# Mixture of experts: token rows fetched and returned by indirect transfers, weights as whole 128-row blocks

## The chip, the cores and the metric

The kernel runs on one core of a Trainium2 chip. The metric is the time on the device in microseconds. Three runs of the kernel before gave 1365.46, 1365.88 and 1366.44 us; the median, 1365.88 us, is what the prediction is measured against. The core's engines work side by side: PE multiplies matrices, ACT and DVE work on elements, POOL (GpSimd) does small vector work and issues transfers that need indices, SP issues the others.

## The reference

256 tokens of 1024 numbers go through two transformer blocks. Nearly all of the change lies in the last part, the second block's mixture of experts, and what it computes is this:

```python
logits = (x @ router_w) + router_b
top_vals, top_idx = lax.top_k(logits, TOP_K)                 # TOP_K = 2 of 8 experts
top_w = jax.nn.softmax(top_vals, axis=-1)
gate = jnp.sum(jax.nn.one_hot(top_idx, N_EXPERTS) * top_w[..., None], axis=-2)
out = jnp.zeros_like(x)
for e in range(N_EXPERTS):
    out = out + gate[..., e:e + 1] * ((jax.nn.silu(x @ w1[e]) * (x @ w3[e])) @ w2[e])
x = layer_norm(DEEPNORM_ALPHA * x + out, ln2_g[1], ln2_b[1])
```

w1 and w3 of an expert have 1024 x 1408 numbers, w2 has 1408 x 1024, all of float32; the eight experts' weights are 138.4 MB. Before this part stand an attention block with a dense hidden layer, a second mixer, a second dense hidden layer and a third mixer; the dense layers and mixers are the first 890 us.

## The kernel before

**Weights.** Every weight is streamed once from DRAM. `Weights.load` (L161) takes the next tile of the plan, up to 4 blocks of 128 rows by 512 columns (1 MB), into a free raw slot, by a transfer that SP issues (L171); the expert part has ten such slots (raw, rawx, cpack, rawt). `Weights.convert` (L175) takes a piece of two row blocks by up to 512 columns and splits it into two parts whose products PE can do fast: ACT rounds it to the high part wh (L204), DVE subtracts to get the low part wl (L205). Six pieces of each part fit (`PIECES`, pools wh and wl). `Weights.pump` is called by `tick` after each piece of products and converts the next pieces as far as `free` allows; a raw slot is free again once DVE has made the last low part from it, and SP waits for that.

**Products.** A product of a block of 128 token slots with 512 columns is three matmuls (`mm3`, L375 to L377: x high by w high, x high by w low, x low by w high). For a block of only 64 slots the high and the low parts of x lie side by side in the 128 columns, and two matmuls do (L1473, L1474); their two halves of rows are added up when the hidden columns are turned (`turn`, L1505).

**Experts.** The router ranks each token among its expert's tokens, and the experts but the first are put in order of their number of tokens, falling ("places" 0 to 6). Blocks run in this order: the first expert (None), then places 4, 1, 5, 2, 3, 6, and at the end place 0 together with an extra block, number 8, of its tokens beyond 128, over the same weights. Places 4 to 6 and block 8 have 64 slots (half), the others 128 (full). The first 384 columns of the first expert are computed for all 256 tokens while the router works.

- `gather` (L1421) collects a block's tokens on PE: a 0/1 matrix Pm (token by slot, made by POOL, L1417) is multiplied with x, in 16 matmuls (L1438), each recorded as two rows; the result is split into xgh and xgl. Pm is also transposed to PT (L1456).
- `expert` (L1459) goes through the columns in chunks of 512, 512 and 384: for each chunk w1 (tiles g), then w3 (tiles u), and the hidden columns are transposed on PE (tp) while the next chunk runs. Then w2 runs by halves of 512 output columns (eacc, `down`), and `rows` (L1555, L1556) scales the result by the gate and splits it into yh and yl.
- `combine` (L1594) multiplies PT with yh and yl and so brings each slot back to its token; the sums of all experts stay in four banks comb, eight matmuls for each block (L1600).

**Order.** Nothing reorders the instructions: they stand as the Python code emits them, and every engine takes its own in order. Side tasks such as `gather` are generators that `tick` advances by a step after so many columns of products.

At the end, DVE adds x and the sums, and a layer norm and the store follow.

Of the kernel before, what the change touches and what calls it, by code (L numbers as in the profile page):

```python
# [28 lines left out]
P = 128  # L29
S = 256  # L30
# [19 lines left out]
def _const_pack():  # L50
# [16 lines left out]
    # distances in the retention: keys of the second block backwards, keys of the first forwards  # L67
# [24 lines left out]
class Null:  # L92
    """Stands for everything on the chip while the order of the weight tiles is listed."""
# [19 lines left out]

class Weights:
    """The weights in the order of their use: raw tiles of up to 512 x 512 by DMA, then in pieces of
    two row blocks an exact pair of float32r parts."""

    def __init__(self, b, plan):
        self.b, self.plan = b, plan
        self.pieces, self.where = [], []  # L120
        for i, (name, r0, kt, c0, n, perm, phase) in enumerate(plan or []):
            for k in range(0, kt, 2):
                self.pieces.append((i, k, min(2, kt - k), n, perm))
                self.where.append(phase)
        # slots of a phase: for the last of its pieces (-phase: in its scratch tiles) and every so many before
# [9 lines left out]
        self.left = {i: (t[2] + 1) // 2 for i, t in enumerate(plan or [])}  # L135
        # makers of raw tiles
        self.slots = deque([lambda: b.rawp.tile([P, 4, 512], F32, name="raw")] * RAW_BUFS)
# [4 lines left out]
    def want(self, name, r0, kt, c0, n, perm=False):  # L142
        """The pieces of a tile, which has to be next in the plan."""
        if self.dry:
            self.list.append((name, r0, kt, c0, n, perm, (self.b.nphase, self.b.extra, self.b.tail)))
            return [(min(2, kt - k), Null(), Null()) for k in range(0, kt, 2)]
        out = []
        for k in range(0, kt, 2):
# [12 lines left out]
    def load(self):  # L161
# [4 lines left out]
        raw = raw[:, :kt, :n]  # L166
# [8 lines left out]
    def convert(self):  # L175
# [5 lines left out]
        if self.where[self.nconv] is None:  # L181
            hi, lo = self.b.wh.tile([P, 2, 512], F32R, name="wh"), self.b.wl.tile([P, 2, 512], F32R, name="wl")
# [50 lines left out]
    def free(self):  # L233
        """Whether there is a slot for the next piece."""
        w = self.where[self.nconv]
        if w is not None and abs(w) != self.b.nphase:
            return False
        n = sum(self.where[i] == w for i in range(self.lag, self.nconv))
        if self.nconv - self.lag >= self.b.ahead:
            return False  # L240
        return n < (PIECES if w is None else self.b.extra if w > 0 else self.b.tail)


class Build:
    def __init__(self, tc, ctx, a, out, stop=None, start=None, plan=None):
# [5 lines left out]
        self.wh = pool("wh", PIECES)  # L251
        self.wl = pool("wl", PIECES)
# [3 lines left out]
        self.ps = pool("ps", 8, space=bass.MemoryType.PSUM)  # L256
        ctx.enter_context(tc.manual_schedule())
# [9 lines left out]
    def weight(self, name):  # L267
        """name: (input, indices...), an index may be a place of the experts' order."""
# [38 lines left out]
    def tick(self, work=1.0):  # L307
        """After a piece of the products; the threads go on once per 6144 columns."""
# [70 lines left out]
    def nat_unit(self, ps, x, t, k0, piece, start, stop):  # L379
        """One token tile through one piece."""  # L380
# [52 lines left out]
    def transposed(self, name, c0, n, x, perm=False, kt=KD):  # L433
        """[col, tok] of n columns: a list of banks holding two column tiles of 128 each."""
# [51 lines left out]
    def vec(self, src, name="vec", eng=None):  # L486
        """A row vector in DRAM on all partitions."""
# [73 lines left out]
    def transition(self, gen, acc, finish, T):  # L561
        """The last products of a part; the first token tile goes on while the second is summed."""
# [18 lines left out]
    def setup(self):  # L581
# [7 lines left out]
        if not self.start:  # L589
            # products of no use, so that the tensor engine's clock is up when those of use come  # L590
# [5 lines left out]
            # the row on all partitions  # L596
# [218 lines left out]
    def nextx(self, x):  # L815
        """The transposed input of the next part, made from x."""
# [156 lines left out]
    def decays(self, l):  # L973
        """The logarithms of the decays of both directions; below 0, for distances that stand for a mask."""
# [9 lines left out]
    def mixer(self, l, xT, T, finish, nextT):  # L984
        """The first token tile of xT is there, T(1) makes the second; finish, nextT: see transition."""
# [11 lines left out]
        # retention values, centred within each head  # L997
# [10 lines left out]
        # queries, keys: columns on the partitions  # L1008
        # of the windowed attention, the high and the low parts one above the other
# [26 lines left out]
        # gates of the merge, gates of the retention, output projections  # L1036
# [38 lines left out]
        def gated(j, name, y):  # L1075
            """A half of the columns of an output, transposed, times twice its gate."""
# [122 lines left out]
    def retention(self, tD, rq, rk, rv, sg, yT):  # L1199
# [5 lines left out]
        for hg in range(2):  # L1205
# [41 lines left out]
    def ret_tail(self, hg, y, sg, yT):  # L1247
        """Norms, gates, and the transposed sum of both directions."""
# [50 lines left out]
    def route_top(self, t, ps):  # L1299
        """The two experts of each token of a tile."""  # L1300
# [303 lines left out]
    def moe(self, x, xT, T):  # L1604
# [33 lines left out]
        def between():  # L1638
            self.route_top(0, g[0][:, n0:])
            T(1)  # L1640
# [211 lines left out]
```

## Time and profile before

| | us |
|---|---|
| median of three runs | 1365.88 |
| span of the profiled execution, first to last instruction | 1364.4 |
| busy: PE / DVE / ACT / POOL | 1329.0 / 971.6 / 769.1 / 126.5 |
| the expert part: routing and first expert | 891.66 to 965.29 |
| places 4, 1, 5, 2, 3, 6 | 965.29 to 1260.41 |
| place 0 and block 8 | 1260.41 to 1348.46 |
| layer norm and store | 1348.46 to 1364.37 |

The profile is of one execution; its span is 1.5 us under the median of the runs, which is what lies around the span. Durations of matmuls overlap in the trace, since the engine takes the next one before the last has ended: what one costs is the distance from its start to the next one's start. The boundaries between the experts are the starts of their first matmuls with w1.

### The profile page before, as it was taken

To read this page: it belongs to the slowest core of one execution; us is meant where nothing else is said; L and a number is where in the kernel's file an instruction comes from. 1 tells how busy PE (TensorE), PEld (TensorE's weight loads), DVE (VectorE), ACT (ScalarE), POOL (GpSimd) and SP (SyncE) were. 2 spreads that over 40 slices of the span, in tenths; PEclk is the share of its full clock that TensorE was granted. 3 is DMA by queue.
4 is the path that set the end of the run, shared out by engine and by line. 5 is a ranking of instruction groups with operands and counts; after the bars stand their busy time and mean duration, and the time that the engine had idled before them with its cause. 6 is when DMAs were issued, how large, how long until landed. Compare 5 with 4: busy or idle time off the path is not lost. (4 is left out here: it accounts for less than half of the span.)

```text
span 1364.4 us, 21025 instructions
## 1 busy us (share of the span) xinstructions
PE 1329.0 (97%) x8214; PEld 1178.8 (86%) x8214; DVE 971.6 (71%) x1287; ACT 769.1 (56%) x1091; POOL 126.5 (9%) x178
## 2 busy tenths in 40 slices
PE   9999999999999999999999999989999999999995
PEld 6977899998998988999979989988878878888893
DVE  6786655556785788455567847778898998889554
ACT  4664644443565545444426645446887887788551
POOL 3401000001001100000010002135100120000000
PEclk9999999999999999999999999999999999999998
DMA  7535656552652555575526624688899999999600
GB/s 271 201 124 169 217 196 223 169 186 77 225 206 64 198 202 201 187 229 185 185 79 190 226 79 149 197 323 303 285 380 355 332 380 347 322 353 381 211 1 33
DMA packets 157269, 294.90 MB, mean 216 GB/s; under 512 B 6201, under 2 KB 33881, under 8 KB 157162
## 3 DMA queue, kind: packets, MB, share of 16 engines
q1 hardware_dynamic: 155322, 287.65, 61.5%
q0 software_dynamic: 1840, 5.83, 1.4%
q8 instruction: 66, 1.08, 0.3%
q14 instruction: 41, 0.34, 0.1%
HBM read 289.26 MB, written 1.05 MB: 213 GB/s over the span
## 5 line engine op out<-in xcount | busy, mean ns | idle before, releaser
L205 DVE TENSOR_TENSOR wl<-raw,wh 128x1024 fp32r<-128x1024 f32 (+2 forms) x346 | 385.8, 1142 | 140.8 <-ACT wh L204 140.0
L204 ACT ACTIVATE wh<-raw 128x1024 fp32r<-128x1024 f32 (+2 forms) x346 | 333.3, 986 | 181.0 <-PE tr L449 109.3
L448 PE MATMUL tr<-xTh,wh 128*128 128x256 f32 x816 | 232.6, 285 | 0.0
L450 PE MATMUL tr<-xTh,wl 128*128 128x256 f32 x816 | 230.9, 283 | 0.0
L449 PE MATMUL tr<-xTl,wh 128*128 128x256 f32 x816 | 230.9, 283 | 0.0
L448 PEld LDWEIGHTS tr<-xTh,wh 128*128 128x128 f32 x816 | 155.7, 191 | 1.2
L449 PEld LDWEIGHTS tr<-xTl,wh 128*128 128x128 f32 x816 | 155.7, 191 | 0.5
L450 PEld LDWEIGHTS tr<-xTh,wl 128*128 128x128 f32 x816 | 155.7, 191 | 0.0
L205 DVE TENSOR_TENSOR wx<-raw,wx 128x1024 fp32r<-128x1024 f32 (+1 forms) x56 | 65.7, 1186 | 52.3 <-ACT wx L204 52.3
L205 DVE TENSOR_TENSOR wl<-rawx,wh 128x1024 fp32r<-128x1024 f32 (+1 forms) x84 | 92.2, 1139 | 6.4 <-ACT wh L204 5.8
L204 ACT ACTIVATE wx<-raw 128x1024 fp32r<-128x1024 f32 (+1 forms) x56 | 56.5, 1026 | 54.6 <-PE tr L449 26.1
L204 ACT ACTIVATE wh<-rawx 128x1024 fp32r<-128x1024 f32 (+1 forms) x84 | 80.1, 987 | 12.3 <-PE g L377 4.3
L449 PE MATMUL tr<-xTl,wx 128*128 128x256 f32 x240 | 67.9, 283 | 0.0
L450 PE MATMUL tr<-xTh,wx 128*128 128x256 f32 x240 | 67.8, 283 | 0.0
L448 PE MATMUL tr<-xTh,wx 128*128 128x256 f32 x240 | 67.3, 280 | 0.0
L483 POOL TENSOR_SCALAR rs<-lnmv 128x1 f32<-128x1 f32 x10 | 7.8, 778 | 597.8 <-DVE lnmv L530 597.8
L375 PE MATMUL nat<-wh,xTh 128*128 128x512 f32 (+1 forms) x152 | 60.4, 397 | 0.4 <-ACT xTh L459 0.4
L376 PE MATMUL nat<-wl,xTh 128*128 128x512 f32 (+1 forms) x152 | 59.0, 388 | 1.0 <-DVE wl L205 0.9
L205 DVE TENSOR_TENSOR wl<-rawt,wh 128x1024 fp32r<-128x1024 f32 (+2 forms) x52 | 56.3, 1116 | 5.1 <-ACT wh L204 4.8
L377 PE MATMUL nat<-wh,xTl 128*128 128x512 f32 (+1 forms) x152 | 58.7, 386 | 0.1
L204 ACT ACTIVATE wh<-rawt 128x1024 fp32r<-128x1024 f32 (+2 forms) x52 | 48.7, 972 | 7.0 <-PE u L377 2.2
L448 PEld LDWEIGHTS tr<-xTh,wx 128*128 128x128 f32 x240 | 45.6, 190 | 0.1
(472 smaller groups left out, 3122.2 us busy)
## 6 DMA issues: line engine op xcount, KB each, us to landing
raw<-in_w_in SPq DMA_DIRECT2D x43, 1024.0 KB, 5.4
raw<-in_moe_w SPq DMA_DIRECT2D x42, 1024.0 KB, 6.8
raw<-in_ffn_w SPq DMA_DIRECT2D x30, 1024.0 KB, 5.2
rawx<-in_moe_w SPq DMA_DIRECT2D x29, 1024.0 KB, 8.4
rawt<-in_moe_w SPq DMA_DIRECT2D x16, 1024.0 KB, 7.1
raw<-in_moe_w SPq DMA_DIRECT2D x20, 768.0 KB, 5.9
raw<-in_w_gate SPq DMA_DIRECT2D x10, 1024.0 KB, 5.1
raw<-in_w_up SPq DMA_DIRECT2D x10, 1024.0 KB, 5.4
```

Of the source, the lines that this page charges most:

```text
L204: nc.scalar.activation(hi[:, :kn, :n], src, AF.Copy)
L205: nc.vector.tensor_sub(lo[:, :kn, :n], src, hi[:, :kn, :n])
L375: mm(out, xh, wh, start=start, stop=False)
L376: mm(out, xh, wl, start=False, stop=False)
L377: mm(out, xl, wh, start=False, stop=stop)
L448: mm(o, a, xh[:, kb + k], start=first and j % 2 == 0, stop=False, **kw)
L449: mm(o, a, xl[:, kb + k], start=False, stop=False, **kw)
L450: mm(o, b, xh[:, kb + k], start=False, stop=(kb + k == kt - 1), **kw)
L483: nc.gpsimd.tensor_scalar(out, ms, eps, None, op0=OP.add)
```

## The change

1. **Weight pieces.** In the expert part a weight tile is now one block of 128 whole rows: 1408 columns of w1 and w3 (0.72 MB), 1024 columns of w2 (0.52 MB). Each is one transfer, one raw slot and one piece for ACT and DVE. The converted parts lie in one ring of 6 x 1024 columns each; a 1408-column piece takes 1536 of it, so four fit. The ten raw slots stay ten. The last pair of blocks (place 0 and 8) keeps chunks of columns, with two row blocks for each transfer.
2. **Fetch.** Blocks 4, 1, 5, 2, 3, 6, 0 and 8 are fetched by `fetch`: PE finds each slot's token number and gate by a product of Pm with two columns (gp), POOL issues one indirect transfer of the token rows from a copy of x in DRAM (xd), and PE transposes these rows in 8 transposes. The first expert's block is gathered as before.
3. **Return.** The result of the first expert and of places 4, 1, 5, 2, 3 and 6 is scaled by ACT and written to a buffer yd in DRAM (ACT issues these transfers; for half blocks POOL adds the second half by an accumulating transfer). When the last pair begins, POOL fetches for each token its two rows of yd, the second added to the first; tokens without such a row get a row of zeros. Only the last pair is still combined on PE. yd is filled with zeros in the first dense layer.
4. **Order.** `whole` takes all columns at once: w1, then w3, then w2 with both output halves. The first 3 (full) or 4 (half) row blocks of the next expert's w1 are put between w3 and w2, and the hidden columns' transposes stand between these.

On PE, between the rows of w1 of place 5, stands in the kernel before the gather of the next block, place 2 (xg is the block's values in columns, x_79 and x_80 are the two token tiles, g the sums with w1):

```order
L1473 MATMUL g<-wh,xgl 128x384
L1474 MATMUL g<-wl,xgl 128x384
L1438 MATMUL xg<-Pm,x_79 128x128
L1438 MATMUL xg<-Pm,x_80 128x128
L1438 MATMUL xg<-Pm,x_79 128x128
L1438 MATMUL xg<-Pm,x_80 128x128
```

Two more such pairs follow there, and four further on. In the changed kernel PE has this at the same place (xrows are the fetched rows, ident the identity):

```order
L1540 MATMUL g<-wh,xgh 128x384
L1541 MATMUL g<-wl,xgh 128x384
L1529 MATMUL xg<-ident,xrows 128x128 x4
L1540 MATMUL g<-wh,xgh 128x512
L1541 MATMUL g<-wl,xgh 128x512
```

Four transposes stand where eight products stood, and they stand behind an indirect transfer that has to have landed.

On ACT, at the end of a half block and in the next expert, stands this in the changed kernel (wh conversions, y the scaled result, sg the first product's activation):

```order
L214 ACTIVATE wh<-rawx 128x1408
L1631 ACTIVATE y<-eacc,gslot 128x512
L1634 DMA yd<-y 64x512
L1631 ACTIVATE y<-eacc,gslot 128x512
L1634 DMA yd<-y 64x512
L214 ACTIVATE wh<-rawx 128x1408 x3
L474 ACTIVATE xgh<-xg 128x4x128
L214 ACTIVATE wh<-raw 128x1408 x2
L474 ACTIVATE xgh<-xg 128x4x128
L1604 ACTIVATE sg<-g 128x512 x2
```

The issue of the results' transfers stands on ACT between conversions; conversions are of 1408 columns where they were of 1024 and 768.

The diff, cut to its core:

```diff
+def rows_of(n):
+    return 2 if n <= 512 else 1
...
+        self.room = [1024 if p[3] <= 512 else 1536 for p in self.pieces]
...
-            hi, lo = self.b.wh.tile([P, 2, 512], F32R, name="wh"), self.b.wl.tile([P, 2, 512], F32R, name="wl")
+            m = self.room[self.nconv]
+            at = self.at if self.at + m <= PIECES * 1024 else 0
+            self.at = at + m
+            hi, lo = (v[:, at:at + m].rearrange("p (k c) -> p k c", k=rows_of(n)) for v in self.b.wparts)
...
+        if w is None:
+            return sum(self.room[i] for i in range(self.lag, self.nconv + 1) if self.where[i] is None) <= PIECES * 1024
...
+        if w1[0] == "w_gate":
+            zero = self.vtile("zero")
+            nc.gpsimd.memset(zero, 0.0)
+            for i in range(NE):
+                nc.gpsimd.dma_start(self.yd[i * P:(i + 1) * P], zero)
+            nc.gpsimd.dma_start(self.yd[NE * P:], zero[:NE])
...
+    def fetch(self, j, out, half=False, back=False):
+        Pm = self.slots([self.prank[:, t, j:j + 1] for t in range(2)], half)
+        yield
+        yield
+        gp = self.bank([2], "gp")
+        for t in range(2):
+            mm(gp, Pm[:, t], self.pg[:, t::5, j], start=(t == 0), stop=(t == 1))
...
+        nc.vector.tensor_copy(ix, gp[:, 1:2])
+        nc.vector.tensor_copy(g, gp[:, 0:1])
...
+        nc.gpsimd.indirect_dma_start(out=v[:w], out_offset=None, in_=self.xd[:, :],
+                                     in_offset=self.rows_at(ix[:w, 0:1]))
+        for _ in range(4):
+            yield
+        for k0 in range(0, KD, 4):
+            for k in range(4):
+                nc.tensor.transpose(ps[:, k], v[:w, (k0 + k) * P:(k0 + k + 1) * P], self.ident[:w, :w])
+            self.split(xh[:, ks, :w], xh[:, ks, 64:] if half else xl[:, ks], ps)
+            yield
...
+    def whole(self, W, blk, w1, w3, w2, place, hT0=None):
+        ahead = 4 if half else 3
+        def row(w, ps, k):
+            (_, wh, wl), = W.want(w, k * P, 1, c0, n)
+            for p, (c, m) in zip(ps, cols):
+                self.mm_block(p, [v if v is None else v[:, k] for v in x], wh[:, 0, c:c + m], wl[:, 0, c:c + m],
+                              k == 0, k == KD - 1)
+            W.done()
+            self.tick(n / (3072 if half else 2048))
...
+        for hf in range(2):
+            y = self.b2([512], "y")
+            nc.scalar.activation(y, acc[hf], AF.Copy, scale=g)
+            if half:
+                nc.scalar.dma_start(self.yd[r0:r0 + 64, sl], y[:64])
+                nc.gpsimd.dma_start(self.yd[r0:r0 + 64, sl], y[64:], accum_op=OP.add)
+            else:
+                nc.scalar.dma_start(self.yd[r0:r0 + P, sl], y)
...
+        for t in range(2):
+            for i in range(2):
+                nc.gpsimd.indirect_dma_start(
+                    out=x2[t], out_offset=None, in_=self.yd[:, :],
+                    in_offset=self.rows_at(self.yrow[:, t, i:i + 1]),
+                    **({"compute_op": OP.add} if i else {}))
```

## Rows read from the trace of the kernel before

**Rows 1.** The page's part 1: busy us, share of the span, instructions.

```profile
PE 1329.0 (97%) x8214; PEld 1178.8 (86%) x8214; DVE 971.6 (71%) x1287; ACT 769.1 (56%) x1091; POOL 126.5 (9%) x178
```

**Rows 2.** Stages: us; PE, PEld, DVE, ACT, POOL busy; PEclk, DMA share, GB/s.

```profile
891.66:965.29 73.63, 69.17 (x377) 60.49 (x377) 58.37 (x100) 43.43 (x57) 30.12 (x59) 1.00 0.82 289
965.29:1010.37 45.08, 42.69 (x231) 36.11 (x230) 41.14 (x46) 39.03 (x53) 7.19 (x4) 1.00 0.99 355
1010.37:1063.26 52.89, 52.89 (x269) 45.56 (x268) 46.43 (x49) 39.29 (x47) 0.00 (x0) 1.00 1.01 354
1063.26:1108.14 44.88, 42.69 (x231) 36.10 (x230) 41.37 (x47) 39.02 (x53) 7.49 (x4) 1.00 0.99 355
1108.14:1161.02 52.88, 52.88 (x268) 45.55 (x267) 46.94 (x49) 39.46 (x47) 6.26 (x2) 1.00 1.01 355
1161.02:1213.89 52.87, 52.87 (x268) 45.54 (x267) 44.95 (x48) 39.03 (x47) 2.71 (x4) 1.00 0.96 335
1213.89:1260.41 46.52, 45.97 (x270) 40.54 (x268) 42.47 (x50) 39.80 (x56) 0.00 (x0) 1.00 1.02 373
1260.41:1348.46 88.05, 87.63 (x426) 74.06 (x424) 49.94 (x57) 41.77 (x56) 0.00 (x0) 1.00 0.26 89
1348.46:1364.37 15.91, 0.00 (x0) 0.00 (x0) 7.96 (x13) 0.00 (x0) 2.70 (x4) 0.59 0.19 70
```

**Rows 3.** PE in order of time near a gather: start, us, instruction, count.

```profile
986.01 1.95 PE L1438 MATMUL xg<-Pm,x 128*128 128x128 f32 x16
987.71 0.42 PE L1473 MATMUL g<-wh,xgl 128*128 128x384 f32 x1
```

**Rows 4.** PE's groups from 840 us to the end: gather and combine.

```profile
L1438 PE MATMUL xg<-Pm,x 128*128 128x128 f32 x160 | 19.6, 275 | 0.5 <-POOL Pm L1417 0.5
L1438 PE MATMUL xg<-Pm,x 128*128 128x64 f32 x128 | 15.4, 272 | 1.0 <-POOL Pm L1417 1.0
L1600 PE MATMUL comb<-yl,PT 128*128 128x512 f32 x36 | 14.6, 406 | 2.2 <-DVE yl L1556 2.2
L1600 PE MATMUL comb<-yh,PT 128*128 128x512 f32 x36 | 14.3, 396 | 0.1
```

**Rows 5.** PE in order of time, the second half of place 4.

```profile
1006.31 0.50 PE L1600 MATMUL comb<-yl,PT 128*128 128x512 f32 x1 [0.98 <-DVE yl L1556]
1006.64 0.39 PE L1600 MATMUL comb<-yh,PT 128*128 128x512 f32 x1
1006.87 0.39 PE L1600 MATMUL comb<-yl,PT 128*128 128x512 f32 x1
```

**Rows 6.** DVE's groups in the six middle experts, 965.29 to 1260.41 us.

```profile
L205 DVE TENSOR_TENSOR wl<-raw,wh 128x1024 fp32r<-128x1024 f32 x67 | 78.9, 1223 | 5.5 <-ACT wh L204 5.2 <-DMA raw<-in_moe_w 0.2
...
L205 DVE TENSOR_TENSOR wl<-raw,wh 128x768 fp32r<-128x768 f32 x16 | 14.6, 952 | 0.8 <-ACT wh L204 0.7
...
L1556 DVE SCALAR_TENSOR_TENSOR yl<-eacc,gslot,yh 128x512 fp32r<-128x512 f32 x12 | 9.0, 749 | 4.2 <-ACT yh L1555 4.2
```

**Rows 7.** Transfers in the six middle experts: queue, then issues with us to landing.

```profile
q1 hardware_dynamic: 55030, 103.14, 98.5%
...
raw<-in_moe_w SPq DMA_DIRECT2D x31, 1024.0 KB, 7.6
...
vec<-in_ln_g POOLq DMA_DIRECT2D x1, 512.0 KB, 8.0
vec<-in_ln_b POOLq DMA_DIRECT2D x1, 512.0 KB, 9.4
```

**Rows 8.** Waits of SP's queue in the same stretch: total us, times, longest.

```profile
SPq L171 <- DVE wl L205: 219.7, 103, 4.5
```

**Rows 9.** Five microseconds inside place 4; columns as in Rows 2.

```profile
990.00:995.00 5.00, 5.00 (x37) 5.00 (x37) 4.00 (x6) 3.70 (x7) 0.00 (x0) 1.00 1.03 390
```

**Rows 10.** POOL in order of time, issuing a transfer of 512 KB.

```profile
1200.46 0.66 POOL L489 DMA_DIRECT2D vec<-in_ln_g  x1
```

**Rows 11.** The first dense layer's first 40 us; columns as in Rows 2.

```profile
137.00:177.00 40.00, 39.75 (x253) 35.83 (x253) 25.69 (x27) 23.46 (x29) 1.06 (x2) 1.00 0.61 207
```

More of the change, by code (lines that the diff above doesn't have):

```diff
@@ L121, in __init__ @@
         for i, (name, r0, kt, c0, n, perm, phase) in enumerate(plan or []):
[L122 to L123 removed]
+            for k in range(0, kt, rows_of(n)):
+                self.pieces.append((i, k, min(rows_of(n), kt - k), n, perm))
                 self.where.append(phase)
@@ L237, in free @@
             return False
-        n = sum(self.where[i] == w for i in range(self.lag, self.nconv))
         if self.nconv - self.lag >= self.b.ahead:
             return False
-        return n < (PIECES if w is None else self.b.extra if w > 0 else self.b.tail)
+        if w is None:
+            return sum(self.room[i] for i in range(self.lag, self.nconv + 1) if self.where[i] is None) <= PIECES * 1024
+        n = sum(self.where[i] == w for i in range(self.lag, self.nconv))
+        return n < (self.b.extra if w > 0 else self.b.tail)
 class Build:
@@ new lines, in rows_at, with mm_block, turned @@
+    def rows_at(self, ix):
+        return ix if self.W.dry else bass.IndirectOffsetOnAxis(ap=ix, axis=0)
+    def mm_block(self, out, x, wh, wl, start, stop):
+        if x[1] is None:
+            self.nc.tensor.matmul(out, x[0], wh, start=start, stop=False)
+            self.nc.tensor.matmul(out, x[0], wl, start=False, stop=stop)
+        else:
+            self.mm3(out, *x, wh, wl, start, stop)
+    def turned(self, half, h, n):
+        nc = self.nc
+        nk = n // P
+        if half:
+            tp = self.bank([2, nk, 64], "tp")
+            for j in range(2):
+                for k in range(nk):
+                    nc.tensor.matmul(tp[:, j, k], h[j][:, k * P:(k + 1) * P], self.ident2,
+                                     start=(j == 0 and k == 0), stop=True, skip_group_check=True)
+            v = self.b1([nk, 64], "hf")
+            nc.scalar.activation(v, tp[:, 0], AF.Silu)
+            nc.vector.tensor_mul(v, v, tp[:, 1])
+            t = self.b2([nk, 2, 64], "hT", F32R)
+            self.split(t[:, :, 0], t[:, :, 1], v)
+            return [(t[:, k].rearrange("p a b -> p (a b)"), None) for k in range(nk)]
+        th, tl = (self.b2([nk, P], f"hT{v}", F32R) for v in "hl")
+        tp = self.bank([nk, P], "tp")
+        for k in range(nk):
+            nc.tensor.transpose(tp[:, k], h[0][:, k * P:(k + 1) * P], self.ident)
+        self.split(th, tl, tp)
+        return [(th[:, k], tl[:, k]) for k in range(nk)]
@@ L1640, in between @@
             T(1)
+            for t in range(2):
+                nc.gpsimd.dma_start(self.xd[t * P:(t + 1) * P], x[t])
         n0 = FFE % 512
@@ L1649, in moe @@
         u = self.natural((names[1], 0, 0), 0, n0, xT, work=0.5)
-        raw = []
-        for tag in ("xTh", "xTl"):
-            raw.append(self.act.tile([P, 4, 512], F32, name="rawt", tag=tag, bufs=2))
-            self.W.slots.append(lambda v=raw[-1]: v)
+        raw = [self.act.tile([P, 2048], F32, name="rawt", tag=tag, bufs=2) for tag in ("xTh", "xTl")]
+        self.W.slots.append(lambda: raw[0])
+        x2 = [raw[1][:, t * D:(t + 1) * D] for t in range(2)]
         while not got:
@@ L1687, in late @@
                 yield
-            for j in js:
-                yield from self.gather(x, columns(self.prank, j), columns(self.pgate, j), got, half=4 <= j <= NE)
-        for p, grp in enumerate(groups):
-            run = self.expert(self.W, [blk[j] for j in grp], *[(n, 0, f"p{places[grp[0]]}" if p else 0) for n in names],
-                              hT0=None if p else hT0)
-            end = p == len(groups) - 1
-            next(run)
-            if p:
-                for t in range(2):
-                    self.combine(t, 1, prev[0], prev[1], comb, p == 1, False)
-            if end:
-                g, b = (self.vec(a[f"ln2_{v}_2"][1]) for v in "gb")
-            new = [] if end else groups[p + 1]
-            got = []
-            if new:
-                js = [places[q] for q in new]
-                tg = self.spawn(late(js, got), 4)
-            ys = next(run)
-            mine = [blk[j] for j in grp]
-            for t in range(2):
-                self.combine(t, 0, mine, ys, comb, p == 0, end)
-                if end:
-                    add(t, 0)
-                    self.ln_half(st[t], x2[t], 0)
-            ys = next(run)
-            if new:
-                self.join(tg)
-                blk.update(zip(new, got))
-            prev = (mine, ys)
@@ L1718, in moe @@
-        for t in range(2):
-            self.combine(t, 1, *prev, comb, False, True)
+            gens = [self.fetch(j, got, half=4 <= j <= NE, back=j in groups[-1]) for j in js]
+            while gens:
+                gens = [v for v in gens if next(v, "end") != "end"]
+                yield
+        run = self.whole(self.W, blk[0], *[(n, 0, 0) for n in names], NE - 1, hT0=hT0)
+        nexts = [[j] for j in order[1:]] + groups
+        fetched = [[] for _ in nexts]
+        tg = self.spawn(late(nexts[0], fetched[0]))
@@ new lines, in moe @@
+        for i, js in enumerate(nexts):
+            got = fetched[i]
+            todo = next(run)
+            self.join(tg)
+            if js is groups[-1]:
+                last = self.expert(self.W, got, *[(n, 0, f"p{js[0]}") for n in names], todo=todo)
+                next(last)
+                for _ in run:
+                    pass
+                break
+            tg = self.spawn(late(nexts[i + 1], fetched[i + 1]))
+            new = self.whole(self.W, got[0], *[(n, 0, f"p{js[0]}") for n in names], js[0])
+            next(new)
+            new.send(todo)
+            for _ in run:
+                pass
+            run = new
@@ new lines, in moe @@
+        g, b = (self.vec(a[f"ln2_{v}_2"][1]) for v in "gb")
+        for t in range(2):
+            for i in range(2):
[3 more added lines that the diff above has]
+                    **({"compute_op": OP.add} if i else {}))
+        mine = got
+        ys = next(last)
+        for t in range(2):
+            for hf in range(2):
+                sl = slice(hf * 512, (hf + 1) * 512)
+                nc.vector.scalar_tensor_tensor(x2[t][:, sl], x[t][:, sl], ALPHA, x2[t][:, sl],
+                                               op0=OP.mult, op1=OP.add)
@@ L1720, in moe @@
+        for t in range(2):
+            self.combine(t, 0, mine, ys, comb, True, True)
+            add(t, 0)
+            self.ln_half(st[t], x2[t], 0)
+        ys = next(last)
+        for t in range(2):
+            self.combine(t, 1, mine, ys, comb, True, True)
             add(t, 1)
```

133 lines of the change are left out of this document (109 added, 24 removed).

## The prediction

> **What bounds the kernel now.** First the page's busy shares: PE is busy 97% of the span, DVE 71%, ACT 56% [rows 1]. A share over the whole span hides stages, so next the expert part by stage [rows 2]. A full block (1010.37 to 1063.26, and two more like it) takes 52.9 us and PE has no idle time in it. A half block takes 45.0 us and PE is idle for 2.3 of them; the last of the three, which gathers two blocks, takes 46.5 with 0.5 idle. The granted clock is at its full 2.4 GHz level in all of these (1.00). So PE's own instructions set the time of this part. But the others are not far behind: in the half blocks DVE is busy 41.1 and 41.4 us of 45, and the transfer engines' share is 0.96 to 1.02 through all six middle experts. That last figure does not make the weights the bound: SP, which issues them, waits 219.7 of these 295.1 us for a raw slot that DVE has still to release [rows 8], so loads stand ready ahead of their use. The reader should see a part with one limiting engine and two more within a tenth of it. What the change takes from PE counts in full only until one of those two is reached.
>
> Before 891 us the order on PE is the same in both kernels, and the ring holds six pieces of 1024 columns as before. New there are only the 4.2 MB of zeros, at about 137 us. PE is busy 39.75 of 40 us then and the transfer engines have a share of 0.61 [rows 11]; at the 390 GB/s of the best window [rows 9] the zeros take 11 us of their time, and 4 MB of weights lie ready in four slots. I cost this at nothing; without that cover it would be at most those 11 us.
>
> **The change on PE.** A gather's 16 rows take from 986.01 to 987.71, 1.70 us, 0.106 each [rows 3]; a block has two such groups, 3.40 us. Rows 4 count 160 and 128 of these records, 288, so nine blocks; the first stays, eight go: 27.2 us. Seven of them stand in the six middle experts (23.8 us), one in the first (3.4). A matmul of combine costs 0.23 us, the distance of two starts [rows 5]. There are 72 [rows 4]; 16 stay at the end, 56 go: 13.0 us, of which 48 in the middle experts (11.2), 4 in the first and 4 in the last (0.9 each). Ten of the transposes for PT go in the middle, 1.1 us at the same 0.106. Added are 8 transposes of fetched rows for each block; the trace has none on such rows, and at the gather's 0.106 each they cost 0.85 us, 5.9 in the middle and 0.85 in the first. The two small columns of gp replace one and cost the same. The products with the weights are the same in number and size.
>
> So the six middle experts, 295.1 us (965.29 to 1260.41), become 295.1 - 23.8 - 11.2 - 1.1 + 5.9 = 264.9 us if PE idles as much as now (5.2 us); without any idle time 259.7. In it a half block would take about 40.5 us and a full one 48.
>
> **DVE and ACT.** By the code an expert has 26 conversions of 1024 columns, 8 of 768 and 2 of 512; at 1223 and 952 ns [rows 6], and 0.67 us for 512 by the same slope of 1.06 ns a column, 40.7 us. Now there are 16 of 1408 (1.63 us by that slope) and 11 of 1024: 39.6 us. The two subtractions for yl, 0.75 each, go as well. DVE's 41.2 us in a half block become 38.6 in 40.5, and 46.4 in a full one become 43.8 in 48: 95% and 91% busy. It fits, but the ring now holds four pieces of 1.63 us where it held six, so that ACT's and DVE's other work shows on PE sooner. I leave PE's present idle time standing for it, although two of its causes go: the wait for yl, 0.98 us [rows 5], and a wait for turned columns, since rows of the next expert's w1 now stand between the transposes. ACT loses yh for y and gets two issues of transfers, at SP's scale a fraction of a microsecond each; it was busy 39 of 45 us and does not decide.
>
> **The transfers.** In the middle experts 103.1 MB came in 295.1 us, 350 GB/s at 98.5% [rows 7]; the best five microseconds had 390 [rows 9]. Now the same span of work needs 103.8 MB of weights and about 6.6 MB more: 2.9 MB of token rows (four full blocks of 0.52 MB, three half ones of 0.26) and 3.7 MB of results (four full, two half ones whose second halves are read and added). At 390 GB/s 110.4 MB take 283 us. The lead shortens that: a load takes 7.6 us to land [rows 7] while one of 1.05 MB passes every 3.0 us, so about 2.5 of ten slots are under way and six hold landed weights; six of 0.72 MB are 4.3 MB, 11 us, that may be used up. So 272 us if rows of 5632 bytes move no faster than rows of 2048, and less than PE's 264.9 if they move 5% faster. No row here shows rows of that length. I take 269, between PE's sum and that floor: 26.1 us saved in the middle. Both ends stay for the range: 259.7 and, with the transfers held to the mean of 350 GB/s, 110.4 / 350 - 11 = 304, nine more than now.
>
> The Trainium skill speaks against this more strongly: "DMA: Bandwidth & Descriptors", section "Where 436 GB/s comes from", puts what HBM gives one core at about 358 GB/s. By it the 110.4 MB would take 308 us, 297 with the lead, and nothing would be won. The trace differs: 390 GB/s in a five-microsecond window and 373 over a whole half block [rows 2, 9]. The same page ("Measured", under "Bandwidth") asks for transfers of 1 MiB, which the change cuts to 0.72 and 0.52 MB; here two or three are always under way, so what one costs alone is hidden.
>
> **The waits that come in.** PE stands at the first transposes of a fetched block until the rows have landed. Between gp and these stand, by the order, 48 to 54 matmuls: 11.2 us at the shortest (48 times 0.23). The chain behind gp is DVE's small copy behind a running conversion (up to 1.2 us), POOL's issue (0.66 us [rows 10]) and the landing; the nearest transfers by POOL, also 0.5 MB and in the same crowd, landed after 8.0 and 9.4 us [rows 7]. Sum 9.9 to 11.3, just covered. Queued behind a late one is all of PE. An indirect transfer is not in this trace; it can be faster than those (then nothing) or slower (a rival below). For the first fetched block, place 4, its transposes come right before its first products, so the chain of transposes, ACT's and DVE's split behind running conversions is bare: 2.5 us, two conversions. On SP each result's transfer takes one of eight semaphores in turn, and a weight load six or seven places behind waits for it; the loads under way cover that.
>
> First expert: 73.6 - 3.4 - 0.9 + 0.85 + 2.5 = 72.7, 0.9 us saved. Last pair: 0.9 saved; the four reads of yd lie beside its 88 us of PE work, where the transfers' share is 0.26 and DVE is busy 50 us, so its 4 extra additions of some 0.75 us are hidden too. The last 15.9 us are unchanged.
>
> **Sum.** 26.1 + 0.9 + 0.9 = 27.9 us. The profiled execution's span of 1364.4 becomes 1336.5, and with the 1.5 us by which the median stands above it, 1338.
>
> **Rivals.**
> 1. PE alone decides: longer rows move fast enough and the stalls go. For it: hardly any wait for weights now. Against: DVE at 95% in half blocks. 259.7 in the middle, 0 for the first chain: 35.4 + 3.4 + 0.9 = 39.7 us, 1326.
> 2. Transfers or conversions hold the part to about half the gain: 370 GB/s gives 110.4 / 370 - 11 = 287, so 8 + 1.8 us won, 1356. For it: share 1.0 already, ten smaller slots instead of ten larger. Against: SP's 219.7 us of waiting for slots.
> 3. The rate stays at the 355 GB/s of the full blocks [rows 2]: 110.4 / 355 - 11 = 300, 4.9 us lost in the middle and 1.8 won elsewhere, 1369. Against it speak the windows of 373 and 390 [rows 2, 9]. This is the mechanism of the rule in the Trainium skill's "DMA: Bandwidth & Descriptors" above, by whose 358 the time would be 1366.
> 4. Fetches land late, the slower side: one mechanism, PE at the eight first transposes. If an indirect transfer takes twice the 8.0 us, the chain is 17.9 us against some 11.7 of cover: 6.2 us each, 50 in all, 1388. It decides once each is over 3.5 us late, that is a landing of 13 us. For it: one descriptor for each token by POOL; against: a half block brings only 0.26 MB.
>
> That the change does not do what it says is not among them: its order shows no gather and no combine in the middle experts.
>
> **Chances.** Forecast 0.55, rival 1 0.14, rival 2 0.17, rival 3 0.06, rival 4 0.08. What this measurement can tell from no change is about 0.2%, 2.7 us. Of rival 2, 0.03 lies so near to no change, and rival 3 straddles the bound, half within and half slower. Faster by more than that: 0.55 + 0.14 + 0.14 = 0.83; within: 0.03 + 0.03 = 0.06; slower: 0.03 + 0.08 = 0.11. The forecast's own range is 1328 to 1349. The range for 8 in 10 goes from 1324, just past rival 1, to 1364 (rival 2 at 362 GB/s), and leaves out rivals 3 and 4 and the nearest part of 2.
>
> **What will show it.** Half blocks of 40 to 42 us and full ones of 48 to 50, no comb before the last pair; PE's waits on DVE's wl in half blocks, small. Rival 2 would show as conversions that wait for loads (ACT or DVE behind DMA), rival 4 as PE's waits on xrows. I am wrong if the six middle experts take under 260 or over 280 us.

## The result: faster, by two thirds of what was forecast

| | before | changed | ratio, 95% interval |
|---|---|---|---|
| median, us | 1366.16 | 1347.34 | 0.9864 (0.985 to 0.9878) |
| profiled span, us | 1364.4 | 1346.5 | |

The change wins 18.8 us; the forecast was 27.9 (1338). The page's busy shares of the changed kernel hardly differ from [rows 1], PE stands at 97% again:

```profile
PE 1306.9 (97%) x7954; PEld 1142.0 (85%) x7954; DVE 959.3 (71%) x1234; ACT 762.1 (57%) x1030; POOL 157.3 (12%) x221
```

The stages, in the columns of [rows 2]: first expert, places 4, 1, 5, 2, 3, 6, last pair, end.

```profile
889.78:968.31 78.53, 73.15 (x374) 63.51 (x375) 62.91 (x107) 47.67 (x57) 41.01 (x78) 0.96 0.74 267
968.31:1011.87 43.56, 41.83 (x201) 31.48 (x199) 38.07 (x36) 36.78 (x43) 1.78 (x1) 1.00 0.96 372
1011.87:1061.44 49.57, 48.68 (x231) 40.21 (x230) 45.31 (x40) 39.42 (x39) 9.37 (x7) 1.00 1.02 401
1061.44:1104.94 43.50, 41.79 (x200) 31.45 (x199) 38.06 (x36) 36.88 (x43) 1.85 (x1) 1.00 1.00 386
1104.94:1154.37 49.43, 49.09 (x234) 40.87 (x233) 44.83 (x39) 38.65 (x38) 13.23 (x9) 1.00 1.02 396
1154.37:1206.24 51.87, 50.33 (x247) 42.06 (x247) 45.49 (x43) 40.48 (x43) 2.45 (x2) 1.00 0.97 369
1206.24:1252.24 46.00, 44.74 (x210) 33.45 (x208) 37.21 (x34) 37.42 (x47) 0.00 (x0) 1.00 0.93 344
1252.24:1330.42 78.18, 77.77 (x382) 65.79 (x380) 48.07 (x58) 36.47 (x51) 8.96 (x8) 1.00 0.60 198
1330.42:1346.50 16.08, 0.00 (x0) 0.00 (x0) 7.95 (x13) 0.00 (x0) 2.71 (x4) 0.55 0.19 69
```

These stages end where an expert's w2 ends on PE, and by then some rows of the next expert's w1 are done, which was not so before. To compare like with like, each such product is put back where it belongs at its full-speed distance (0.21 us on the mean of 512 and 384 columns, 0.23 at 512): 24 products before a half block, 27 before a full one, 40 before the last pair. For place 4 that is 43.56 + 5.1 - 5.7. In us:

| | before | forecast | changed |
|---|---|---|---|
| half blocks, places 4 and 5 | 45.1, 44.9 | 40.5 | 43.0, 42.9 |
| place 6 | 46.5 | | 42.0 |
| full blocks, places 1, 2, 3 | 52.9 each | 48 | 50.2, 49.4, 52.5 |
| the six | 295.1 | 269 | 279.9 |
| first expert | 73.6 | 72.7 | 73.4 |
| last pair | 88.05 | 87.2 | 87.3 |

The remaining 1.9 us are from before 891 us, where PE's order is the same. They build up in small steps from the start on; I know no cause, and four runs of the changed kernel lie 4.5 us apart.

Place 3 is longer than the other full blocks by what stands in it for the last pair: 1.7 us of PE's work for that pair's two fetches, and a wait of 0.9 us for fetched rows. In the kernel before, these two blocks were gathered in place 6.

So the loss against the forecast is in the half blocks, and in smaller part in the full ones. PE's busy column doesn't show it: place 4 has 1.7 us idle. The reason is in how matmuls are recorded. This is PE in order of time in place 4's w2 (start, us, instruction):

```profile
1005.25 0.50 PE L1541 MATMUL eacc<-wl,hT 128*128 128x512 f32 x1
1005.59 0.40 PE L1540 MATMUL eacc<-wh,hT 128*128 128x512 f32 x1
1005.83 0.40 PE L1541 MATMUL eacc<-wl,hT 128*128 128x512 f32 x1
1006.07 0.39 PE L1540 MATMUL eacc<-wh,hT 128*128 128x512 f32 x1
1006.52 0.50 PE L1541 MATMUL eacc<-wl,hT 128*128 128x512 f32 x1
1006.86 0.40 PE L1540 MATMUL eacc<-wh,hT 128*128 128x512 f32 x1
```

A product lasts 0.40 us, the next starts after 0.23. From 1006.07 to 1006.52 the distance is 0.45: PE waited, but 0.39 of it count as busy. Distances of starts above those at full speed, added up, are PE's lost time; it is an estimate, and the choice of the full-speed distance moves each total by a few us, before and after alike. In the six middle experts it is 11.1 us before and 27.4 now: 9.6 in the half blocks' w3 (0.7 before), 5.5 in their w2 (2.9), 9.5 in w1 of both sorts with the transposes between its rows (4.0), 2.8 elsewhere (3.5, of it 2.4 in combine).

What PE waits for, by the waits from 968.31 to 1252.24 us (total, times, longest; PEld is the load that PE makes ahead of a product, at which the product's wait then shows):

```profile
DVE wl L215 <- ACT wh L214: 25.5, 44, 2.1
ACT hf L1557 <- PE tp L1554: 13.8, 9, 2.5
...
PEld u L1541 <- DVE wl L215: 11.5, 24, 1.3
PEld eacc L1541 <- DVE wl L215: 8.9, 24, 0.5
...
ACT wh L214 <- DMA rawx<-in_moe_w: 2.4, 4, 1.1
```

PE waits for DVE's low parts (wl); the conversions hardly wait for a load. DVE in place 4, in order of time, shows why a unit that is busy for 38 of 43.6 us can be the limit:

```profile
987.25 5.82 DVE L215 TENSOR_TENSOR wl<-rawx,wh 128x1408 fp32r<-128x1408 f32 x4
993.07 0.42 DVE L1558 TENSOR_TENSOR hf<-hf,tp 128x256 f32<-128x256 f32 x1
993.97 0.43 DVE L475 TENSOR_TENSOR hT<-hf,hT 128x256 fp32r<-128x256 f32 x1 [0.48 <-ACT hT L474]
994.92 1.23 DVE L215 TENSOR_TENSOR wl<-raw,wh 128x1024 fp32r<-128x1024 f32 x1 [0.52 <-ACT wh L214]
...
1006.38 4.62 DVE L215 TENSOR_TENSOR wl<-rawx,wh 128x1024 fp32r<-128x1024 f32 x4
```

In w3 a row takes DVE about 1.53 us (starts at 982.65, 984.18, 985.72, 987.25), PE six products, 1.27 at full speed (four distances of 0.23 and two of 0.175). In w2 it takes 4.62 / 4 = 1.16, PE 0.93. In the turning between (993 to 1002) the chain PE, ACT, DVE, ACT, DVE of hf and hT holds both converters; ACT stands 13.8 us there, in the nine turnings of the three half blocks. What PE can run ahead is the ring: four rows of 1408.

The sums say the same once lost time is left out. At full speed PE's instructions in place 4 would take about 37 us, and DVE is busy for 38.07. Before, it was about 40.5, gather and sums included, and DVE was busy for 41.14 [rows 2]: in half blocks DVE had not been the shorter of the two even then.

### The profile page after: what moved, and what is told of

It is laid out like the page before. It is cut to its first block, busy times and chain, and to the rows that moved or that the text cites. A ratio compares the mean times of both kernels' runs of the same rounds, so it can differ in the third digit from the quotient of the medians.

```text
span 1346.5 us, 20822 instructions
## 1 busy us (share of the span) xinstructions
PE 1306.9 (97%) x7954; PEld 1142.0 (85%) x7954; DVE 959.3 (71%) x1234; ACT 762.1 (57%) x1030; POOL 157.3 (12%) x221
## 3 DMA queue, kind: packets, MB, share of 16 engines
q8 instruction: 64, 1.05, 0.3%
## 5 line engine op out<-in xcount | busy, mean ns | idle before, releaser
L215 DVE TENSOR_TENSOR wl<-raw,wh 128x1024 fp32r<-128x1024 f32 (+3 forms) x322 | 379.8, 1203 | 139.4 <-ACT wh L214 138.3
L214 ACT ACTIVATE wh<-raw 128x1024 fp32r<-128x1024 f32 (+3 forms) x322 | 327.4, 1037 | 173.7 <-PE tr L464 100.5
L215 DVE TENSOR_TENSOR wl<-rawx,wh 128x1024 fp32r<-128x1024 f32 (+2 forms) x90 | 120.8, 1373 | 15.4 <-ACT wh L214 14.9
L214 ACT ACTIVATE wh<-rawx 128x1024 fp32r<-128x1024 f32 (+2 forms) x90 | 103.5, 1180 | 15.6 <-PE eacc L392 5.3
L215 DVE TENSOR_TENSOR wx<-raw,wx 128x1024 fp32r<-128x1024 f32 (+1 forms) x56 | 65.5, 1185 | 49.4 <-ACT wx L214 49.4
L463 PEld LDWEIGHTS tr<-xTh,wx 128*128 128x128 f32 x240 | 45.3, 189 | 0.1
L464 PEld LDWEIGHTS tr<-xTl,wx 128*128 128x128 f32 x240 | 45.2, 188 | 0.1
L465 PEld LDWEIGHTS tr<-xTh,wx 128*128 128x128 f32 x240 | 45.3, 189 | 0.0
```

What stands on the lines that cost most here:

```text
L214: nc.scalar.activation(hi[:, :kn, :n], src, AF.Copy)
L215: nc.vector.tensor_sub(lo[:, :kn, :n], src, hi[:, :kn, :n])
L463: mm(o, a, xh[:, kb + k], start=first and j % 2 == 0, stop=False, **kw)
L464: mm(o, a, xl[:, kb + k], start=False, stop=False, **kw)
L465: mm(o, b, xh[:, kb + k], start=False, stop=(kb + k == kt - 1), **kw)
```

## The experiments

Each was timed against the kernel before on the same chip; the changed kernel is at 0.9864. Theory A is the above: in half blocks PE goes at the pace of the conversions.

**1. e1_relief: less work for DVE in half blocks**

```diff
-            nc.vector.tensor_sub(lo[:, :kn, :n], src, hi[:, :kn, :n])
+            q = 512 if self.plan[i][0][-1] in ("p4", "p5", "p6") else n
+            nc.vector.tensor_sub(lo[:, :kn, :q], src[:, :, :q], hi[:, :kn, :q])
```

> Leaves out: in the three half blocks DVE makes the low part of a weight row for the first 512 columns only, and the products read these 512 for every column group. PE's and ACT's instructions and all transfers stay. Theory A (in the half blocks PE runs at DVE's pace: a w3 row is 1.53 us of DVE for 1.36 of PE, a w2 row 1.14 for 0.93): the half blocks fall from 43.5 to about 38 us, the total by 14 to 17, to 1330 to 1334. Theory B (the transfers hold the part, 107 MB at 378 GB/s, share near 1.0): no change, 1347, and at the most the 272 us that I worked out as their floor, 10 us less, 1337; ACT's conversions would then wait for loads. Theory C (SP's loads are late because they wait for semaphores that the results' transfers hold): no change, 1347.

1332.89 us, 0.9756 (0.974 to 0.9772). Places 4 and 5, in the columns of the stages:

```profile
962.73:1003.15 40.42, 38.81 (x201) 32.13 (x199) 23.52 (x35) 35.02 (x42) 1.47 (x1) 1.00 0.99 392
...
1052.82:1093.90 41.08, 38.98 (x200) 32.08 (x199) 23.62 (x35) 35.37 (x42) 1.53 (x1) 1.00 1.02 409
```

Put back as above these are 39.8 and 40.5 us, what the forecast had for a half block, and the six take 270.3. PE's lost time falls from 27.4 to 17.7, that of the half blocks' w2 from 5.5 to 0.4. So the part of DVE's work that this run leaves out of the half blocks costs the 14.5 us. In what is left in w3 (6.1) PE waits 3.5 us for wl and 2.6 for wh, and DVE itself stands behind ACT, which takes 1.27 us a row, as much as PE, and has the splits between.

**2. e2_noreturn: no results returned.** The transfers of the results at the end of `whole` are taken out. ACT's scaling stays, other than the expectation says: its trace has all 14 activations of y.

> Leaves out: the first expert and the six middle blocks don't write their results (no scaling by ACT, no transfer to DRAM), the reads at the end stay. 3.7 MB less and SP's 42 us of waits for those transfers gone. Theory A: under 1 us, 1346 to 1348. Theory B: 3.7 MB at 378 GB/s, 9.8 us less, 1337. Theory C: about 10 us less too, 1337, with PE's waits for DVE gone.

1344.56 us, 0.9840 (0.9824 to 0.9857), 2.8 less, nearer to A than to the 9.8 of theory B; the intervals don't tell it from nothing. SP's waits for the results' transfers, 42.3 us in the changed kernel, were gone, and its waits for raw slots grew from 110.6 to 174.3: the loads were early enough either way. The bytes of the six experts hardly fell (107.26 MB for 107.46), because POOL's reads of yd, which wait for no results here, come from 1210 us on and no longer in the last pair. What fewer bytes do shows in the first five of the six, changed kernel and this run:

```profile
968.31:1206.24 237.93, 231.72 (x1108) 186.07 (x1107) 211.75 (x190) 192.21 (x202) 28.68 (x20) 1.00 0.99 385
967.58:1205.33 237.75, 231.86 (x1108) 186.57 (x1107) 212.56 (x191) 192.33 (x203) 26.86 (x17) 1.00 0.98 378
```

89.9 MB and not 91.6 went through in the same time, at a lower rate: the transfers don't set it.

**3. e3_pieces: the DRAM part alone.** Fetch and return as changed, `expert` with its pieces as before (with nine raw slots of 1 MB, where the kernel before had ten):

```diff
-        run = self.whole(self.W, blk[0], *[(n, 0, 0) for n in names], NE - 1, hT0=hT0)
...
+            run = self.expert(self.W, got, *[(n, 0, f"p{js[0]}" if i else 0) for n in names],
+                              hT0=None if i else hT0, place=js[0] if i else NE - 1)
```

> The DRAM part of the change alone: rows fetched and results returned through DRAM, but the weights in pieces of 2 x 512 columns and loads of 4 x 512, chunk by chunk, as in the kernel before. Theory A: PE loses the gathers and sums (a full block 48.4 us), a half block is DVE's 39.7 us and its stalls, 42 to 43.5: 275 us in the middle, 1340 to 1348, so the whole rows bring nothing of their own. Theory B with the prediction's view that long rows move faster: the middle at the 355 GB/s of the full blocks before, 1360 to 1369.

1344.35 us, 0.9842 (0.9826 to 0.9859): 3.0 less than the whole change, within the intervals. So the whole rows and their order bring nothing that can be told; the gain is that of the DRAM part. Places 1, 5, 2, 3:

```profile
1007.69:1056.14 48.45, 48.45 (x235) 40.81 (x234) 45.32 (x50) 39.69 (x48) 10.95 (x7) 1.00 1.06 376
1056.14:1099.14 43.00, 39.67 (x197) 31.05 (x196) 38.09 (x43) 36.42 (x50) 1.82 (x1) 1.00 1.05 386
1099.14:1147.96 48.82, 48.67 (x234) 40.97 (x233) 46.34 (x50) 40.85 (x49) 10.81 (x7) 1.00 1.06 384
1147.96:1196.39 48.43, 48.43 (x235) 40.83 (x233) 43.16 (x48) 38.71 (x46) 8.31 (x5) 1.00 1.05 381
```

Full blocks take the 48 of the forecast, place 5 43 again, but for another reason (place 4 has 44.5 at a granted clock of 0.90, place 6 44.1). Of 26.1 us lost in the middle 12.2 are in the half blocks' w2, and half of these at one place in each of the three, where the turned columns come late (the whole rows cover this with rows of the next w1):

```profile
PE eacc L1654 <- DVE hT L475: 6.1, 3, 2.0
```

So the whole rows mend that wait and lose as much to the conversions. Their w3 loses 1.8 us and not 9.6.

**4. e6_gather: the gather on PE again**

```diff
-                nc.tensor.transpose(ps[:, k], v[:w, (k0 + k) * P:(k0 + k + 1) * P], self.ident[:w, :w])
+                for t in range(2):
+                    mm(ps[:, k], self.gx[t][:, (k0 + k) * P:(k0 + k + 1) * P], Pm[:, t, :w],
```

> The fetch undone, the rest of the change kept: the rows are gathered by 32 products on PE as before, no rows come from DRAM. 7 blocks times 2.55 us more of PE in the middle, 17.9, and 2.9 MB less to transfer. If PE has no slack: 1365. Theory A: the four gathers that stand in half blocks hide in part behind DVE, 10 to 14 us more, 1357 to 1361. Theory B: transfers relieved, PE's time hidden, 0 to 5 more, 1347 to 1352.

1354.9 us, 0.9921 (0.9905 to 0.9938): 7.6 more for about 18 us more of PE's work. The six go from 283.9 to 293.9 us as they stand, PE's lost time falls from 27.4 to 20.0. Products that need no weights let DVE catch up. It is somewhat below A's range because place 4's stall in the first expert (experiment 7) is gone as well: from 938 to 948 us PE is busy for 9.16 us, at the full clock.

**5. e5_small: one row less in the ring.** The limit of the converted ring is 5 x 1024 columns in the expert part.

> The converted ring of the expert part holds 5 x 1024 columns and not 6: three rows of 1408 ahead and not four, with the same memory, transfers and instructions. Theory A: a half block lives on the rows that were converted ahead during the full block before it; one row less of w1 or w3 is 1.5 us of DVE's lead, lost two to three times in the three half blocks: 3 to 7 more, 1350 to 1354. If the transfers hold the part, the ring is of no matter: 1347 to 1348.

1360.15 us, 0.9957 (0.994 to 0.9973), 12.8 more: far more than A's 3 to 7. PE loses 39.1 us in the middle; not the half blocks alone need those four rows (full blocks' w1 and w3 lose 9.6 us, 4.9 in the changed kernel). The loads are not what it waits for: conversions stand 1.0 us for them in all, and the six move 365 GB/s at a share of 0.96.

**6. e4_mix: half blocks' w2 mixed with the next w1**

```diff
+            if mix and k >= 1 and k % 2:
+                mix.popleft()()
```

> The same work in another order: in each block's w2 a row of the next block's w1 that is still to come stands behind every second w2 row, so that PE's short rows of half blocks (0.93 us for 1.14 of DVE) stand beside long ones of full blocks (1.92 for 1.53). Theory A (DVE's pace in half blocks, with a conversion ring that covers four to six rows): the 1.9 us that a half block's w2 loses, and part of the wait behind it, go: 5 to 8 less, 1339 to 1342. If the loss is one of sums and not of order (transfers, or DVE over the whole part): 1347.

1350.29 us, 0.9883 (0.9866 to 0.9899), 3.0 more, which the intervals just don't tell from nothing. The half blocks' w2 loses 2.2 us and no longer 5.5, as A said, but w3 loses 12.0 (9.6), and the full blocks' w3 4.5 (0.7): the long rows that were mixed in are missing where they refilled the ring. A is right about the place and wrong that this order mends it.

**7. e7_early and h3_pieces7early: place 4's fetch earlier.** In the changed kernel PE stands at the first fetched rows (PE in order of time, then two windows):

```profile
938.81 0.71 PE L1529 MATMUL xg<-ident,xrows 64*128 64x64 f32 x8
943.55 0.80 PE L1540 MATMUL g<-wh,xgl 128*128 128x512 f32 x1 [4.03 <-DVE xgl L475]
...
938.80:943.50 4.70, 0.73 (x9) 0.58 (x8) 3.92 (x8) 2.06 (x4) 4.19 (x7) 0.94 1.03 411
943.50:948.00 4.50, 4.45 (x13) 3.77 (x14) 3.43 (x7) 0.84 (x2) 1.45 (x4) 0.50 0.87 327
```

The rows are there; the split on DVE stands behind two conversions. And after 4 us without work the granted clock is 0.50, the 1.2 GHz level: twelve products take 0.42 us each and not 0.21, 2.5 us more.

```diff
-        yield
+        if j != 4:
+            yield
```

> Place 4's fetch goes one step earlier (some 2.7 us of PE's work), so that its transposes stand among the first expert's w3 rows and not before their own first use. By the view that PE's 4.0 us there are the bare chain behind the transposes, and the 3 us after it the clock that fell to half: both shrink, 4 to 6 less, 1341 to 1343. If the landing of the rows decides instead, they are then late at the transposes: 0 to 1 less, 1346 to 1347.

1345.75 us, 0.9848 (0.9832 to 0.9865), 1.6 less, which the intervals don't tell from nothing. The first wait is gone, and the next stands behind it:

```profile
945.15 0.63 PE L1566 MATMUL tp<-ident,sg 128*128 128x128 f32 x4 [2.82 <-DVE sg L1618]
```

> As h1_pieces7, and place 4's fetch spawned two steps earlier, so that its transposes stand some 5 us earlier, inside the first expert's w2. In e3 PE stood 2.3 us there and ran some 5 us at half the clock, 2.6 us lost. If nothing else is late behind it, 4 to 5 less than h1; if another wait takes its place, as in e7, 1 to 2 less.

1352.11 us beside 1352.26 for h1_pieces7: no gain either.

**8. e9_pool: POOL makes every fourth low part of the half blocks**

```diff
+            helps = self.plan[i][0][-1] in ("p4", "p5", "p6") and self.plan[i][1] // P % 4 == 1
+            (nc.gpsimd if helps else nc.vector).tensor_sub(lo[:, :kn, :n], src, hi[:, :kn, :n])
```

> In the half blocks POOL, and not DVE, makes the low part of every fourth row (7 of 27). Takes 9.5 us from DVE's 38 in a half block. Theory A: if POOL needs up to about 4 us a row, 8 to 14 less, as far as the ring covers POOL's longer time: 1333 to 1340. If POOL needs 6 us or more, PE waits for it instead and the time is 1347 or more. Theory B: 1347.

1368.76 us, 1.002 (1.0009 to 1.0031), 21 more. POOL and then DVE in place 4:

```profile
976.45 3.21 POOL L216 TENSOR_TENSOR wl<-rawx,wh 128x1408 fp32r<-128x1408 f32 x1 [4.69 <-PE g L1542]
983.36 4.51 POOL L216 TENSOR_TENSOR wl<-raw,wh 128x1408 fp32r<-128x1408 f32 x1 [3.70 <-ACT wh L214]
```

```profile
977.68 5.00 DVE L216 TENSOR_TENSOR wl<-raw,wh 128x1408 fp32r<-128x1408 f32 x2 [0.52 <-ACT wh L214]
...
984.74 4.62 DVE L216 TENSOR_TENSOR wl<-cpack,wh 128x1408 fp32r<-128x1408 f32 x1
```

POOL needs 3.2 us for a row, as hoped. But DVE's subtraction that begins at 984.74 ends 1.5 us after POOL's at 987.87: it lasts 4.62 us and not 1.62. What POOL took off DVE came back as standing time: in the six DVE's 144 subtractions take 232.7 us, where 162 took 225.9. The Trainium skill states this ("SBUF — State Buffer", section "SBUF: two separate sides"): POOL and a DVE operation with two inputs in SBUF lock a shared port pair for a whole instruction, and the other one stands. The trace agrees; the row at 984.74 (4.62 us) is just that. And PE waits 16.1 us for the rows that POOL makes.

**9. h1_pieces7 and h2_ring5: a larger ring for fewer raw slots.** The new slot lies in the expert part's own scratch memory.

```diff
-        self.phase("moe", 0, 14, 7, ahead=99, rawx=[
+        self.phase("moe", 0, 14, 7, ahead=99, extra=1, rawx=[
```

> The kernel of e3 (rows and results through DRAM, weights in pieces of 2 x 512) with a seventh slot of 1024 columns in the converted ring of the expert part, in the memory of one raw slot (eight raw slots, not nine). Theory A2 (PE and the DVE/ACT pair run at nearly the same rate and lose time to each other for want of a buffer between them; a row less cost 12.8 us): 4 to 7 less than e3, 1337 to 1340. If transfers hold it, the lost raw slot counts and the ring doesn't: 1344 or more.

> The changed kernel with a fifth slot for a row of 1408 columns in the converted ring, in the memory of two raw slots (eight, not ten). Theory A2: the fourth row was worth 12.8 us, the fifth some 4 to 8: 1339 to 1343. If transfers hold it: 1347 or more.

1352.26 (0.9893, 0.9877 to 0.991) and 1360.42 (0.9959, 0.9946 to 0.9973): slower than their bases. Some 8 us arise before the middle experts: the router's weights go into the new slot, which can be filled only once the scratch memory of the part before is free. PE in h1_pieces7:

```profile
896.40 1.02 PE L428 MATMUL nat<-wx,xTh 128*128 128x392 f32 x2 [6.88 <-POOL wx L205]
```

In the middle h1 loses 26.7 us (e3: 26.1) and h2 33.6, with more waits for loads than in the changed kernel (9.2 us of ACT, 3.0 there). What a fifth row alone would bring stays open.

**10. h4_reliefnoreturn: e1 and e2 together**

> Leaves out both what e1 leaves out (low parts beyond 512 columns in the half blocks) and what e2 leaves out (the results' transfers, 3.7 MB). e1's six middle experts took about 272 us, which is also the transfer floor of the prediction. If the transfers hold e1 there, 3.7 MB less are 9 us less: 1323 to 1325. If they don't, as e2's 2.8 us say: 1330 to 1331.

1330.53 us, 0.9738 (0.9722 to 0.9754), 2.4 below e1, as e2 had it and within the intervals. But it doesn't decide what it was made for. The six experts of e1 and of this run:

```profile
962.73:1236.99 274.26, 267.56 (x1317) 221.73 (x1315) 197.03 (x223) 227.16 (x246) 27.84 (x20) 1.00 1.00 390
962.62:1233.70 271.08, 266.75 (x1316) 222.06 (x1315) 197.18 (x223) 226.28 (x245) 27.65 (x22) 1.00 1.01 390
```

As in e2 the reads of yd move into the six, so the bytes fall by 1.3 MB and not by 3.7, and the time falls with them at the same 390 GB/s. Whether transfers hold part of e1's 270 us stays open. Against it: e1's conversions wait 3.1 us for loads in all, and SP waits 93.0 us for raw slots. Only e1 and this run, which leave DVE's work out, are faster than the changed kernel by more than the intervals.

## Why the prediction was right in sign and a third too high

- **PE's sum** (295.1 - 23.8 - 11.2 - 1.1 + 5.9): right. The changed middle holds 256.5 us of products at full speed; 4.0 of these belong to the last pair on balance, so 252.5, and before it was 284.0: 31.5 less, where I had 30.2.
- **"I leave PE's present idle time standing for it"**: this is the step that failed. I took 5.2 us; the lost time, counted by distances of starts, was 11.1 and became 27.4. I had DVE at 95% in a half block and wrote that it fits. It fits into the 40.5 us only because PE's idle time is in them; PE's own products take about 37, less than DVE's 38. DVE and ACT stand in the turning as well, and w3 and w2 are then run at 1.53 and 1.16 us a row where PE needs 1.27 and 0.93. The gathers that the change removes were time in which DVE caught up: e6 puts them back and gets 7.4 of their 18 us for nothing. That the sums were so too was not tested. e1 frees DVE and gets the half blocks of the forecast.
- **"269, between PE's sum and that floor"**: my 4 us for transfers stood in the right place by accident. The transfers moved 107.46 MB at 378 GB/s and up to 401 in a full block, at a share of 1.02, where it had been 354 at 1.01 [rows 2]. That they don't decide is shown by the conversions, which wait 3.0 us for loads in all, by e5, and by e2's first five experts. The 358 GB/s of the Trainium skill ("DMA: Bandwidth & Descriptors", section "Where 436 GB/s comes from") is not the limit in this trace.
- **Full blocks 48 us**: right in e3 (48.4 to 48.8); 49.4 and 50.2 in the changed kernel, and 52.5 in place 3 with its extra work. That full blocks are longer because the ring is refilled there is my reading; no run tests it alone.
- **The waits that come in**: right for the fetches; transposes waited once for rows, 0.9 us, and they landed after 9.3 (below); POOL's issue took 1.65 us where I had 0.66. Place 4's bare chain was 4.0 us and not 2.5, and I had not counted the clock behind it; two waits of the first expert went (1.6 us for DVE's xgh, 1.5 for POOL's Pm), so the stage is 0.7 us off. SP's 42.3 us of waiting behind the results are covered by loads under way, as said.
- **Last pair, end**: as said, within 0.2 us. The stages before 891 us, where the zeros are written, did not get longer; they are 1.9 us shorter, for no cause that I know.

```profile
rawx<-in_moe_w SPq DMA_DIRECT2D x33, 704.0 KB, 11.5
raw<-in_moe_w SPq DMA_DIRECT2D x31, 704.0 KB, 8.1
...
xrows<-xd,islot POOLq DMA_INDIRECT x6, 9.3
```

Of the rivals the second was nearest in kind (conversions keep part of the gain), but its sign, conversions that wait for loads, was absent (3.0 us in all). Its 1356 lies 9 us from the measured time, as far as my 1338. That the time fell into the range doesn't bear out the sum: the 4 us that I kept for transfers stood for a loss of another kind, four times as large. By my own signs, the six at 279.9 are at the edge of 260 to 280, places 4 and 5 (43), 1 (50.2) and 3 (52.5) lie outside theirs, and PE's waits for wl in half blocks, which I expected to be small, are the larger part of the loss.

## What to carry to other kernels

Taking work off the bounding engine pays only where the next engine has slack in that very stretch: compare the two per row (here 1.53 against 1.27 us, 1.16 against 0.93), leave lost time out of the sums of a block (38 against 37), and ask whether the removed work was what the next engine used to catch up. Two engines at nearly the same pace live on the buffer between them; here the loss of one row of four cost 12.8 us, two thirds of what the whole change had won. And read a matmul engine by distances of starts, since its busy time hides short waits.

## What the runs showed of the hardware

- A stand of 4.0 us on PE cost another 2.5 us: the granted clock was 0.50 in the next 4.5 us (the 1.2 GHz level), after 0.94 in the 4.7 us of the stand.
- A POOL subtraction of 1408 columns takes 3.2 us at best, and a DVE one that begins beside it stands until it ends: 4.62 us for 1.62 (e9_pool).
- An indirect fetch of 0.26 to 0.5 MB lands 9.3 us after its issue (median of six), like POOL's plain transfers of 0.5 MB in [rows 7] (8.0 and 9.4), and its issue holds POOL for 1.65 us against 0.66 in [rows 10].
- Transfers of whole rows moved 396 to 401 GB/s over a full block at a share of 1.02. Rows of 2048 bytes moved 354 before at 1.01, but 381 to 386 in e3's blocks 5, 2 and 3 at 1.05 and 1.06, so the length of the rows is at most part of the difference.
